# A decoder block's feed-forward down product: 16 of 22 row tiles by Strassen's seven block products, with sums of weight blocks kept in DRAM

## The chip, the cores and the metric

One core of one Trainium2 chip runs the whole kernel in one launch. The time is device time in microseconds. Before the change the median of three runs is 962.39 us, lowest 961.94 and highest 962.43. The engines are named as the profile names them: PE (TensorE), DVE (VectorE), ACT (ScalarE), POOL (GpSimd) and SP (SyncE, which here only issues DMAs).

## The reference

One layer of a hybrid decoder block for 512 tokens of width 1024, everything in float32:

```python
mod = cs @ ada_w[l] + ada_b[l]                       # cs = silu(c)
sh_m, sc_m, gt_m, sh_f, sc_f, gt_f = jnp.split(mod, N_MOD, axis=-1)
h = modulate(rmsnorm(x, norm_mix_g[l]), sh_m, sc_m)
proj = h @ w_in[l]                                   # q k v g_ret b_cv c_cv u_cv g_a g_b
...
y_a = (jax.nn.silu(g_ret) * y_ret) @ ret_w_out[l]    # retention branch
y_b = (b_cv * conv) @ conv_w_out[l]                  # short convolution branch
merged = jax.nn.sigmoid(g_a) * y_a + jax.nn.sigmoid(g_b) * y_b
x = x + gt_m[:, None, :] * (merged @ mix_w_out[l])
h = modulate(rmsnorm(x, norm_ffn_g[l]), sh_f, sc_f)
f = (jax.nn.silu(h @ ffn_w_gate[l]) * (h @ ffn_w_up[l])) @ ffn_w_down[l]
x = x + gt_f[:, None, :] * f
return rmsnorm(x, final_norm_g)
```

The feed-forward is 2816 wide, which is 22 row tiles of 128 of `ffn_w_down`. The change concerns the last matrix product, `f`, and when the vector `gt_f` is made.

## The kernel before

Each float32 operand is split into a high and a low part (`w_..._h`, `w_..._l`), and each product is three matmuls: low by high, high by low, high by high. A weight goes through four steps. SP's queue loads 1 MB into a `raw` buffer (`load_raw`, tag "raw", three buffers for the whole kernel); ACT casts a half of it to the high part; DVE subtracts to get the low part (`split`: tags "hi" and "lo", four buffers each); PE multiplies. SP's DMAs are issued in one order (`issue_after(load_raw.last...)`), so a load that waits for a free buffer holds back all behind it.

The stages of the code that matter here, in their order:

- The merge, two loops of four steps. A step of the first loop has the products `p_ga` and `p_ya` (loads `w_ga`, `w_ya`) and a part of the modulation for the feed-forward: `ada_load` fetches two buffers `ada_f` in eight DMAs of 256 KB, `mod_vecs` sums their rows on DVE (`acc_f`, eight operations) and four short matmuls turn the sum into columns. A step of the second loop has `p_gb` and `p_yb` (loads `w_gb`, `w_yb`). In its first step `gate_vec("gt_m")` starts: in four pieces, 1 MB of `ada_gt_m` is summed over rows on DVE (`acc_gt_m`, eight operations), split (`gh`, `gl`), and spread over the partitions by two matmuls (`gp_gt_m`). The pieces are taken at later points of the code (`after`, `tick`).
- `mix`: the merged product with `mix_w_out`, the residual sum into `x1` (`dx_gt_m`), and the feed-forward's norm, whose order is written out by hand on PE, DVE and ACT (`strict`): `n2s` to `n_r`, its reciprocal, `xn`, transposes `tx`, `h`, `Gh` and `Gl`.
- The feed-forward in two parts of 12 and 10 row tiles (`PARTS`). `swiglu` yields two tiles of silu(gate) × up for each 1 MB of `w_fg` and of `w_fu`; each tile is split (`fa_h`, `fa_l`). `tm_gemm` then multiplies them, tokens on the output's partitions, with two halves of 512 columns of `ffn_w_down` (`w_dn`, four row tiles in 1 MB) into four PSUM banks `dn`, and `add_gated` multiplies by `gt_f` and adds to `x1`. `gate_vec("gt_f")` starts at the third pair of tiles of the first part.

Of the kernel before, what the change touches and what calls it, by code (L numbers as in the profile page):

```python
# [19 lines left out]
P = 128  # L20
# [50 lines left out]
def block_kernel(ctx, tc, x, c, positions, ada_w, ada_b, norm_mix_g, w_in, conv_w, ret_w_out,  # L71
# [165 lines left out]
    def mod_vecs(f, j):  # L237

        pt = aux(f"mod_{f}{j}")
        a = ada_sum(ada_raw.pop((f, j)), 4 * P, f"{f}{j}")  # L240
        for i in range(4):
            mm(pt[:, i:i + 1], lhsT=a[:, i * P:(i + 1) * P], rhs=ones32[:, 0:1],
               start=True, stop=True)
        mod_cols(f, j, pt)
# [541 lines left out]
    def gate_vec(name):
        gate[name] = [misc(f"{name}_{h}") for h in range(2)]
        for h in range(2):
            with tc.issue_after(load_raw.last.ins):
                nc.sync.dma_start(  # L790
                    gate[name][h],
                    ada_b[0, ADA[name] + h * S:ADA[name] + (h + 1) * S].partition_broadcast(P))
        parts = {}

        def summed(j):
            raw = wp.tile([P, KT, 2 * P], F32, tag="raw", bufs=3, name=f"ada_{name}{j}")
            col = ADA[name] + 2 * j * P
            load_raw.last = nc.sync.dma_start(raw, aw[:, :, col:col + 2 * P])
            a = ada_sum([raw[:, k] for k in range(KT)], 2 * P, f"{name}{j}")
            gh = sp.tile([P, 2 * P], F32R, tag="gh", bufs=1, name=f"gh_{name}{j}")  # L800
            gl = sp.tile([P, 2 * P], F32R, tag="gl", bufs=1, name=f"gl_{name}{j}")
            parts[j] = split_act(a, "", gh, gl)

        def spread(j):
            gh, gl = parts.pop(j)
            pt = aux(f"gp_{name}{j}")
            mm(pt[:, 0:2 * P], lhsT=onesr, rhs=gl, start=True, stop=False)
            mm(pt[:, 0:2 * P], lhsT=onesr, rhs=gh, start=False, stop=True)
            gv = gate[name][j // 2][:, (j % 2) * 2 * P:(j % 2 + 1) * 2 * P]
            vec.tensor_tensor(gv, gv, pt[:, 0:2 * P], ALU.add)  # L810

        for j in range(4):
            after(2 * j + 1, lambda j=j: summed(j))
            after(2 * j + 2, lambda j=j: spread(j))

    for p in range(KT // 2):
        sg = {}
        for i, pt in proj(wi, COL["gb"] + 2 * p * P, Hh, Hl, f"gb{p}"):
            sg[i] = scr(f"sgb{p}{i}")
            act.activation(sg[i], pt, AF.Sigmoid)  # L820
        for i, pt in proj(conv_w_out[0], 2 * p * P, conv_in, None, f"yb{p}"):
# [48 lines left out]
    def add_gated(t, h, pt, g, cs=slice(0, S)):  # L870
        d = scr(f"dx_{g}{t}{h}_{cs.start}")[:, cs]
        vec.tensor_tensor(d, pt[:, cs], gate[g][h][:, cs], ALU.mult)
        vec.tensor_tensor(x1[t][h][:, cs], x1[t][h][:, cs], d, ALU.add)
# [133 lines left out]
    def swiglu(col):  # L1007
        if col == 0:
            for i, pg, pu in first_ffn():
                g = scr(f"fg{col}_{i}")  # L1010
                act.activation(g, pg, AF.Silu)
                vec.tensor_tensor(g, pu, g, ALU.mult)
                yield split_act(g, f"fa{i}")
            return
        gg = {}
        for i, pt in proj(ffn_w_gate[0], col, Gh, Gl, f"fg{col}"):
            gg[i] = scr(f"fg{col}_{i}")
            act.activation(gg[i], pt, AF.Silu)
        for i, pt in proj(ffn_w_up[0], col, Gh, Gl, f"fu{col}"):
            vec.tensor_tensor(gg[i], pt, gg[i], ALU.mult)  # L1020
            yield split_act(gg[i], f"fa{col}_{i}")

    o2 = out[0].rearrange("(t p) (h n) -> t h p n", p=P, n=S)
    ss3 = [sp.tile([P, 3], F32, tag="ss3", name=f"nfs_{t}") for t in range(NT)]
    PARTS = ((0, 12), (12, 10))
    for part, (f0, nf) in enumerate(PARTS):
        af = []
        for q in range(nf // 2):
            af += swiglu((f0 + 2 * q) * P)
            if part == 0 and q == 2:  # L1030
                gate_vec("gt_f")
        for h in range(2):
            groups = [acc(f"dn{part}{h}_{t}") for t in range(NT)]
            if part == 1 and h == 0:
                fg = [misc(f"fg_{i}") for i in range(2)]
                for i in range(2):
                    with tc.issue_after(load_raw.last.ins):
                        nc.sync.dma_start(
                            fg[i], final_norm_g[i * S:(i + 1) * S].partition_broadcast(P))
            if part == 0 or h == 0:  # L1040
                for t in tm_gemm(ffn_w_down[0], af, f0, nf, h, groups, nf - 4, f"dn{part}"):
                    add_gated(t, h, groups[t], "gt_f")
                    if part == 1:
                        half_ss(x1[t][h], ss3[t], h, f"nf_{t}")
                        vec.tensor_scalar(ss3[t][:, 0:1], ss3[t][:, 0:1], 1.0 / D, EPS, ALU.mult,
                                          ALU.add)
                        vec.tensor_tensor(x1[t][h], x1[t][h], fg[h], ALU.mult)
                continue
            groups.append(aux("dn_last"))
            xg = {}  # L1050
            for t, cs in tm_gemm(ffn_w_down[0], af, f0, nf, h, groups, nf - 6, f"dn{part}", True):
                add_gated(t, h, groups[NT if cs.start else t], "gt_f", cs)
                half_ss(x1[t][h][:, cs], ss3[t], 1 + cs.start // HS, f"nf_{t}")
                if cs.start == 0:
                    xg[t] = scr(f"xg_{t}")
                if cs.stop < S:
                    vec.scalar_tensor_tensor(ss3[t][:, 0:1], ss3[t][:, 1:2], 1.0 / D,
                                             ss3[t][:, 0:1], ALU.mult, ALU.add)
                vec.tensor_tensor(xg[t][:, cs], x1[t][h][:, cs], fg[h][:, cs], ALU.mult)
                if cs.stop < S:  # L1060
                    continue
                r = sp.tile([P, 1], F32, tag="rr", name=f"nf_{t}_r")
                i = 1 + cs.start // HS
                act.activation(r, ss3[t][:, i:i + 1], AF.Sqrt, scale=1.0 / D, bias=ss3[t][:, 0:1])
                vec.reciprocal(r, r)
                for i in (1, 0):
                    o = scr(f"o_{t}{i}")
                    if i:
                        vec.tensor_scalar_mul(o, xg[t], r)
                    else:  # L1070
                        act.mul(o, x1[t][0], r)
                    (nc.sync if i or t < NT - 1 else nc.scalar).dma_start(o2[t, i], o)


# [33 lines left out]
```

## Time and profile before

| | before |
|---|---|
| median of 3 runs | 962.39 us |
| the profiled execution's own time | 962.06 us |
| its span | 960.3 us |
| TensorE's granted clock, mean | 0.998 |
| PE busy | 949.9 us, 99% |
| DVE busy | 555.9 us, 58% |
| ACT busy | 340.1 us, 35% |
| POOL busy | 10.1 us, 1% |
| DMA, mean over the span | 126 GB/s |

Busy time is what an engine spends in instructions; shares are of the span. Times of instructions are counted from the span's start. The chain of work that ended last is followed back from the last instruction, and a row of it gives a start, a length, the engine, the tile written, the line and how many instructions in a row. DMA rows give the size of one transfer and the median time from its issue to its landing; the name before "DMA_DIRECT2D" is the queue that issued it.

### The profile page before, as it was taken

The page shows a single profiled execution, that of the slowest core. Times are in us where ns is not written, and L with a number is a line of the kernel's source. Part 1 is how long each engine was busy: PE and PEld are TensorE (multiplying, and loading weights), DVE is VectorE, ACT ScalarE, POOL GpSimd, SP SyncE. Part 2 cuts the span into 40 slices and gives each one's busy share as a digit, 9 for nine tenths or more (in the row PEclk, how much of TensorE's full clock was granted, in tenths as well). Part 3 has the DMA queues.
Part 4 walks back from the last instruction along what each step waited for, and adds up shares of the span by engine and source line. Part 5 has one row for each costly group of instructions (what it writes and reads, how often), then busy time and mean ns, then how long its engine had stood idle before and what let it go on. Part 6 is the DMA issues. An engine that isn't in the chain of part 4 may idle for free.

```text
span 960.3 us, 11325 instructions
## 1 busy us (share of the span) xinstructions
PE 949.9 (99%) x4619; PEld 802.7 (84%) x4619; DVE 555.9 (58%) x843; ACT 340.1 (35%) x505; POOL 10.1 (1%) x20
## 2 busy tenths in 40 slices
PE   8999999999999999999999999999999999999997
PEld 8898889888888888888888888888888888888886
DVE  5988875959674855554574358346533443333354
ACT  7534434444443423222232336333222122322223
POOL 2002000000000000000000000000000000000000
PEclk9999999999999999999999999999999999999999
DMA  9944223141222246764553640445433223332302
GB/s 308 343 146 133 80 96 99 56 143 56 88 88 88 77 127 189 209 188 154 175 175 101 206 132 15 140 132 175 133 116 103 87 88 93 122 114 66 110 1 88
DMA packets 109045, 120.98 MB, mean 126 GB/s; under 512 B 3701, under 2 KB 96929, under 8 KB 108993
## 3 DMA queue, kind: packets, MB, share of 16 engines
q1 hardware_dynamic: 108624, 119.82, 39.8%
q8 instruction: 36, 0.59, 0.3%
q0 software_dynamic: 224, 0.18, 0.1%
q10 hardware_dynamic: 144, 0.26, 0.1%
q14 instruction: 17, 0.13, 0.0%
HBM read 118.15 MB, written 2.10 MB: 125 GB/s over the span
## 4 chain that ended last, share of the span: by engine, by line
PE 96%; DVE 2%; ACT 1%; DMA 1%; issue 0%; SPq 0%; ACTq 0%
PE p_fu L64 13%; PE p_fg L64 12%; PE dn L64 12%; PE p_v L64 5%; PE p_ga L64 5%; PE p_gb L64 5%; PE p_yb L64 5%; PE p_ya L64 5%; PE p_k L64 4%; PE p_q L64 4%; PE p_g L64 3%; PE p_u L64 3%; PE p_b L64 3%; PE p_c L64 3%; PE mix L64 3%; PE mix L62 2%
## 5 line engine op out<-in xcount | busy, mean ns | idle before, releaser
L64 PE MATMUL dn<-w_dn_h,fa_l 128*128 128x512 f32 (+1 forms) x176 | 67.5, 384 | 0.0
L64 PE MATMUL dn<-w_dn_l,fa_h 128*128 128x512 f32 (+1 forms) x176 | 67.5, 383 | 0.0
L64 PE MATMUL dn<-w_dn_h,fa_h 128*128 128x512 f32 (+1 forms) x176 | 67.4, 383 | 0.0
L64 PE MATMUL p_fu<-Gh,w_fu_l 128*128 128x512 f32 x160 | 62.3, 389 | 0.0
L64 PE MATMUL p_fg<-Gh,w_fg_l 128*128 128x512 f32 x160 | 62.3, 389 | 0.0
L64 PE MATMUL p_fg<-Gh,w_fg_h 128*128 128x512 f32 x160 | 62.3, 389 | 0.0
L64 PE MATMUL p_fu<-Gh,w_fu_h 128*128 128x512 f32 x160 | 62.3, 389 | 0.0
L64 PE MATMUL p_fg<-Gl,w_fg_h 128*128 128x512 f32 x160 | 62.2, 389 | 0.0
L64 PE MATMUL p_fu<-Gl,w_fu_h 128*128 128x512 f32 x160 | 62.2, 389 | 0.0
L64 DVE TENSOR_TENSOR w_dn_l<-w_dn,w_dn_h 128x1024 fp32r<-128x1024 f32 x22 | 26.9, 1225 | 57.3 <-ACT w_dn_h L64 57.3
L64 DVE TENSOR_TENSOR w_fg_l<-w_fg,w_fg_h 128x1024 fp32r<-128x1024 f32 x20 | 24.4, 1224 | 56.5 <-ACT w_fg_h L64 56.5
L64 ACT CAST w_fu_h<-w_fu 128x1024 fp32r<-128x1024 f32 x20 | 21.1, 1053 | 74.2 <-PE p_fu L64 41.8
L64 ACT CAST w_dn_h<-w_dn 128x1024 fp32r<-128x1024 f32 x22 | 23.1, 1049 | 65.6 <-PE dn L64 39.4
L64 DVE TENSOR_TENSOR fg<-p_fu,fg 128x512 f32<-128x512 f32 x22 | 15.2, 691 | 49.6 <-PE p_fu L64 49.6
L64 ACT ACTIVATE fg<-p_fg 128x512 f32<-128x512 f32 x22 | 13.2, 598 | 78.0 <-PE p_fg L64 78.0
L64 PEld LDWEIGHTS dn<-w_dn_h,fa_l 128*128 128x128 f32 x176 | 33.1, 188 | 6.7 <-DVE dx_gt_f L64 0.2
L64 PEld LDWEIGHTS dn<-w_dn_h,fa_h 128*128 128x128 f32 x176 | 33.1, 188 | 6.5
L64 PEld LDWEIGHTS dn<-w_dn_l,fa_h 128*128 128x128 f32 x176 | 33.1, 188 | 6.4
L64 PE MATMUL p_v<-w_v_h,Hh 128*128 128x256 f32 x128 | 36.2, 283 | 0.0
L64 PE MATMUL p_v<-w_v_l,Hh 128*128 128x256 f32 x128 | 36.2, 283 | 0.0
L64 PE MATMUL p_v<-w_v_h,Hl 128*128 128x256 f32 x128 | 36.2, 283 | 0.0
L64 PEld LDWEIGHTS p_fg<-Gh,w_fg_h 128*128 128x128 f32 x160 | 30.0, 188 | 6.3
(373 smaller groups left out, 2536.1 us busy)
## 6 DMA issues: line engine op xcount, KB each, us to landing
w_fg<-in_ffn_w_gate_dram SPq DMA_DIRECT2D x11, 1024.0 KB, 5.5
w_fu<-in_ffn_w_up_dram SPq DMA_DIRECT2D x11, 1024.0 KB, 5.5
w_dn<-in_ffn_w_down_dram SPq DMA_DIRECT2D x10, 1024.0 KB, 5.1
ada_m<-in_ada_w_dram SPq DMA_DIRECT2D x32, 256.0 KB, 6.0
ada_f<-in_ada_w_dram SPq DMA_DIRECT2D x32, 256.0 KB, 4.9
w_v<-in_w_in_dram SPq DMA_DIRECT2D x4, 1024.0 KB, 6.8
w_q<-in_w_in_dram SPq DMA_DIRECT2D x4, 1024.0 KB, 5.1
w_g<-in_w_in_dram SPq DMA_DIRECT2D x4, 1024.0 KB, 5.1
```

The costliest lines, as they stand in the source:

```text
L62: self.last = op(*args, **kw)
L64: self.last = op(*args, **kw)
```

## The change

The 22 row tiles are now done in three parts of 8, 8 and 6. For the first two, the product A·B (A the activations, B the weights) is cut into 2 × 2 blocks: 256 tokens by four row tiles of A, four row tiles by 512 columns of B. Seven block products stand for eight, with sums of blocks of A (s1 to s4) and of B (t1 to t4) as factors, and sums of the products (u2, u3) on the way to the output. The last six tiles go the old way.

The sums of B don't depend on the data, but on the weights alone; they are made in the merge loops: each of the eight steps loads two row tiles of `ffn_w_down` into a `raw` buffer (`w_bl`), takes four differences on DVE in place, and writes the buffer to DRAM (`blocks`) by a DMA of POOL's queue. Eight of the fourteen block products then load their weights from `blocks`, six from `ffn_w_down`. The sums of A are made on DVE as the second half of a part's tiles comes out of `swiglu`. `gate_vec("gt_f")` starts after the first pair of tiles in place of the third.

```diff
+    dp = ctx.enter_context(tc.tile_pool(name="dp", bufs=1, space=bass.MemoryType.DRAM))
...
+    PARTS = ((0, 8), (8, 8), (16, 6))
+    blocks = [dp.tile([P, nf // 2, 2, D], F32, tag="blocks", bufs=2, name=f"blocks{i}")
+              for i, (_, nf) in enumerate(PARTS[:2])]
+
+    def block_sums():
+        for part, (f0, nf) in enumerate(PARTS[:2]):
+            for k in range(nf // 2):
+                w = wp.tile([P, 2, D], F32, tag="raw", bufs=3, name=f"w_bl{part}{k}")
+                for i in range(2):
+                    r0 = (f0 + k + i * nf // 2) * P
+                    with tc.issue_after(load_raw.last.ins):
+                        load_raw.last = nc.sync.dma_start(w[:, i], ffn_w_down[0, r0:r0 + P, :])
+                (b11, b12), (b21, b22) = ([w[:, i, j * S:(j + 1) * S] for j in range(2)]
+                                          for i in range(2))
+                vec.tensor_tensor(b11, b12, b11, ALU.subtract)
+                vec.tensor_tensor(b12, b22, b12, ALU.subtract)
+                vec.tensor_tensor(b22, b22, b11, ALU.subtract)
+                vec.tensor_tensor(b21, b21, b22, ALU.subtract)
+                nc.gpsimd.dma_start(blocks[part][:, k], w)
+                yield
+
+    block_steps = block_sums()
...
         ada_load("f", 2 * p)
         mod_vecs("f", 2 * p)
+        next(block_steps)
...
         if p == 0:
             gate_vec("gt_m")
+        next(block_steps)
...
+    def block_acts(part, nf):
+
+        first, acts = [], {n: [] for n in ("a11", "a12", "a22", "s1", "s2", "s3", "s4")}
+        tok = slice(0, HS), slice(HS, S)
+        f0 = PARTS[part][0]
+        for q in range(nf // 2):
+            for g in swiglu((f0 + 2 * q) * P):
+                if len(first) < nf // 2:
+                    k = len(first)
+                    t = misc(f"a11_{part}{k}", F32R)
+                    acts["a11"].append(split_act(g[:, tok[0]], "", t[:, tok[0]], t[:, tok[1]]))
+                    first.append(g)
+                    continue
+                k = len(acts["s1"])
+                a11, a21 = (first[k][:, i] for i in tok)
+                a12, a22 = (g[:, i] for i in tok)
+                sums = [scr(f"s{part}{k}_{i}") for i in range(2)]
+                (s1, s2), (s3, s4) = ([s[:, i] for i in tok] for s in sums)
+                both = [split_act(g, f"a2_{part}{k}")]
+                vec.tensor_tensor(s1, a21, a22, ALU.add)
+                vec.tensor_tensor(s2, s1, a11, ALU.subtract)
+                vec.tensor_tensor(s3, a11, a21, ALU.subtract)
+                vec.tensor_tensor(s4, a12, s2, ALU.subtract)
+                both += [split_act(s, f"s{part}{k}{i}") for i, s in enumerate(sums)]
+                for i, n in enumerate(("a12", "a22", "s1", "s2", "s3", "s4")):
+                    acts[n].append([z[:, tok[i % 2]] for z in both[i // 2]])
+            if part == 0 and q == 0:
+                gate_vec("gt_f")
+        return acts
+
+    def block_weights(part, n):
+
+        f0, nf = PARTS[part]
+        h = nf // 2
+        t = {"t1": (0, 0), "t3": (0, 1), "t4": (1, 0), "t2": (1, 1)}.get(n)
+        if t is None:
+            i, j = int(n[1]) - 1, int(n[2]) - 1
+            raw = load_raw(ffn_w_down[0], f0 + i * h, h, j * S, S, f"w_{n}{part}")
+        else:
+            raw = wp.tile([P, h, S], F32, tag="raw", bufs=3, name=f"w_{n}{part}")
+            with tc.issue_after(load_raw.last.ins):
+                load_raw.last = nc.sync.dma_start(
+                    raw, blocks[part][:, :, t[0], t[1] * S:(t[1] + 1) * S])
+        ws = [split(raw[:, k:k + 2, :], [P, 2, S], f"w_{n}{part}{k}") for k in range(0, h, 2)]
+        return [[w[:, k % 2, :] for w in ws[k // 2]] for k in range(h)]
+
+    def block_product(pts, acts, ws):
+        h = len(ws)
+        for i, pt in enumerate(pts):
+            ts = slice(i * P, (i + 1) * P)
+            for k, ((ah, al), (wh, wl)) in enumerate(zip(acts, ws)):
+                mm(pt, lhsT=al[:, ts], rhs=wh, start=k == 0, stop=False)
+                mm(pt, lhsT=ah[:, ts], rhs=wl, start=False, stop=False)
+                mm(pt, lhsT=ah[:, ts], rhs=wh, start=False, stop=k == h - 1)
+            yield i, pt
+
+    def add_gated_sum(t, h, pt, u):
+        d = scr(f"du_{t}{h}")
+        vec.tensor_tensor(d, pt, u, ALU.add)
+        vec.tensor_tensor(d, d, gate["gt_f"][h], ALU.mult)
+        vec.tensor_tensor(x1[t][h], x1[t][h], d, ALU.add)
+
+    def block_down(part, acts):
+
+        def product(bank, a, w):
+            pts = [bank(f"dn{part}_{w}{i}") for i in range(2)]
+            yield from block_product(pts, acts[a], block_weights(part, w))
+
+        u2, u3 = {}, {}
+        for i, pt in product(acc, "a11", "b11"):
+            u2[i] = scr(f"u2_{part}{i}")
+            act.copy(u2[i], pt)
+        for i, pt in product(acc, "a12", "b21"):
+            add_gated_sum(i, 0, pt, u2[i])
+        for i, pt in product(pv, "s2", "t2"):
+            vec.tensor_tensor(u2[i], pt, u2[i], ALU.add)
+        for i, pt in product(aux, "s3", "t3"):
+            u3[i] = scr(f"u3_{part}{i}")
+            vec.tensor_tensor(u3[i], pt, u2[i], ALU.add)
+        for i, pt in product(acc, "s1", "t1"):
+            add_gated_sum(2 + i, 1, pt, u3[i])
+            vec.tensor_tensor(u2[i], pt, u2[i], ALU.add)
+        for i, pt in product(acc, "s4", "b22"):
+            add_gated_sum(i, 1, pt, u2[i])
+        for i, pt in product(pv, "a22", "t4"):
+            add_gated_sum(2 + i, 0, pt, u3[i])
...
-    PARTS = ((0, 12), (12, 10))
-    for part, (f0, nf) in enumerate(PARTS):
-        af = []
-        for q in range(nf // 2):
-            af += swiglu((f0 + 2 * q) * P)
-            if part == 0 and q == 2:
-                gate_vec("gt_f")
...
+    for part in range(2):
+        block_down(part, block_acts(part, PARTS[part][1]))
+
+    f0, nf = PARTS[2]
+    af = []
+    for q in range(nf // 2):
+        af += [split_act(g, f"fa{q}") for g in swiglu((f0 + 2 * q) * P)]
...
```

The last part is the old loop body for one part, with its names shortened. Three places show how this moves instructions. In each row there are the source line, the operation, the tile written, the tiles read, the shape, and how many alike follow each other.

SP's queue in the first steps of the first merge loop, before (`w_ya` in four DMAs, `ada_f` in eight):

```order
L107 DMA w_ga_3294<-in_w_in_dram 128x8x256
L764 DMA w_ya_3358<-in_ret_w_out_dram 64x4x256 x4
L64 DMA ada_f_0_3423<-in_ada_w_dram 128x2x256 x4
L64 DMA ada_f_4_3428<-in_ada_w_dram 128x2x256 x4
L107 DMA w_ga_3450<-in_w_in_dram 128x8x256
L764 DMA w_ya_3514<-in_ret_w_out_dram 64x4x256 x4
L64 DMA ada_f_0_3579<-in_ada_w_dram 128x2x256 x4
```

The same place now:

```order
L108 DMA w_ga_3298<-in_w_in_dram 128x8x256
L791 DMA w_ya_3362<-in_ret_w_out_dram 64x4x256 x4
L64 DMA ada_f_0_3427<-in_ada_w_dram 128x2x256 x4
L64 DMA ada_f_4_3432<-in_ada_w_dram 128x2x256 x4
L756 DMA w_bl_3454<-in_ffn_w_down_dram 128x1024 x2
L108 DMA w_ga_3462<-in_w_in_dram 128x8x256
L791 DMA w_ya_3526<-in_ret_w_out_dram 64x4x256 x4
L64 DMA ada_f_0_3591<-in_ada_w_dram 128x2x256 x4
```

Each block's load stands behind the step's `ada_f` and ahead of the next step's `w_ga`; the next step's first `ada_f` buffer is the one that the block is written from. In the second loop a block's load stands ahead of the next `w_gb`, and the last one ahead of the first `w_mix`.

DVE at the first token tile of the feed-forward's norm (`n2s` holds the sums of squares, `n_0_r` the root), before:

```order
L62 TENSOR_TENSOR x_0_1_4543<-x_0_1_4543,dx_gt_m_0_4770 128x512
L62 TENSOR_TENSOR n_0_r<-n2s_4560 128x1
L62 RECIPROCAL n_0_r<-n_0_r 128x1
L62 TENSOR_SCALAR xn_00_4779<-x_0_0_4542,n_0_r 128x512
L62 TENSOR_SCALAR xn_01_4781<-x_0_1_4543,n_0_r 128x512
```

And now:

```order
L62 TENSOR_TENSOR x_0_1_4611<-x_0_1_4611,dx_gt_m_0_4838 128x512
L62 TENSOR_TENSOR n_0_r<-n2s_4628 128x1
L64 TENSOR_SCALAR acc_gt_f_5295<-ada_gt_f_5293,cs 128x256
L64 SCALAR_TENSOR_TENSOR acc_gt_f_5295<-ada_gt_f_5293,cs,acc_gt_f_5295 128x256 x3
L62 RECIPROCAL n_0_r<-n_0_r 128x1
L64 SCALAR_TENSOR_TENSOR acc_gt_f_5295<-ada_gt_f_5293,cs,acc_gt_f_5295 128x256
L62 TENSOR_SCALAR xn_00_4847<-x_0_0_4610,n_0_r 128x512
L62 TENSOR_SCALAR xn_01_4849<-x_0_1_4611,n_0_r 128x512
```

Sums of the first piece of `gt_f` stand between the steps of the norm, and with them the wait for `ada_gt_f` to land.

DVE at the end of the first part's tiles, where the first block products begin (`fg` a tile of silu(gate) × up, `s` sums of A, `w_b` weights from `ffn_w_down`, `w_t` weights from `blocks`):

```order
L64 TENSOR_TENSOR w_b_l<-w_b_5834,w_b_h 128x1024
L64 TENSOR_TENSOR s_l<-s_1_5727,s_h 128x512
L64 TENSOR_TENSOR fg_1_5692<-p_fu_5748,fg_1_5692 128x512
L64 TENSOR_TENSOR s_0_5774<-fg_1_5337,fg_1_5692 128x256
L64 TENSOR_TENSOR s_1_5775<-fg_1_5337 128x256
L64 TENSOR_TENSOR s_0_5774<-s_0_5774,fg_1_5337 128x256
L64 TENSOR_TENSOR a_03_l<-fg_1_5692,a_03_h 128x512
L64 TENSOR_TENSOR s_1_5775<-fg_1_5692,s_0_5774 128x256
L64 TENSOR_TENSOR s_l<-s_0_5774,s_h 128x512
L64 TENSOR_TENSOR w_b_l<-w_b_5834,w_b_h 128x1024
L64 TENSOR_TENSOR s_l<-s_1_5775,s_h 128x512
L64 TENSOR_TENSOR w_t_l<-w_t_5878,w_t_h 128x1024 x2
```

And at the end of that part's block products:

```order
L64 TENSOR_TENSOR w_t_l<-w_t_6046,w_t_h 128x1024
L64 TENSOR_TENSOR x_0_1_4611<-x_0_1_4611,du_6024 128x512
L64 TENSOR_TENSOR du_6040<-dn_b_6001,u_01_5830 128x512
L64 TENSOR_TENSOR w_fg_l<-w_fg_6088,w_fg_h 128x1024
L64 TENSOR_TENSOR du_6040<-du_6040,gt_f_5257 128x512
L64 TENSOR_TENSOR du_6068<-dn_t_6044,u_00_5938 128x512
L64 TENSOR_TENSOR x_1_1_4613<-x_1_1_4613,du_6040 128x512
```

The splits of the first two products' weights stand among the last tiles of gate and up (the first product's two just ahead of the rows shown), and the splits of the next gate and up weights among the last sums; before, the same place has two operations (`dx_gt_f`, `x`) for each of eight output tiles, and the splits of `w_dn`.

More of the change, by code (lines that the diff above doesn't have):

```diff
@@ L1012, in swiglu @@
                 vec.tensor_tensor(g, pu, g, ALU.mult)
-                yield split_act(g, f"fa{i}")
+                yield g
             return
@@ L1020, in swiglu @@
             vec.tensor_tensor(gg[i], pt, gg[i], ALU.mult)
-            yield split_act(gg[i], f"fa{col}_{i}")
+            yield gg[i]
+    def block_acts(part, nf):
[26 more added lines that the diff above has]
+        return acts
@@ L1023, in block_kernel @@
     o2 = out[0].rearrange("(t p) (h n) -> t h p n", p=P, n=S)
     ss3 = [sp.tile([P, 3], F32, tag="ss3", name=f"nfs_{t}") for t in range(NT)]
-    PARTS = ((0, 12), (12, 10))
-    for part, (f0, nf) in enumerate(PARTS):
-        af = []
-        for q in range(nf // 2):
-            af += swiglu((f0 + 2 * q) * P)
-            if part == 0 and q == 2:
-                gate_vec("gt_f")
[L1032 to L1047, printed above, removed]
-                continue
[L1049 to L1072, printed above, removed]
@@ new lines, in block_kernel @@
+    for part in range(2):
[4 more added lines that the diff above has]
+        af += [split_act(g, f"fa{q}") for g in swiglu((f0 + 2 * q) * P)]
+    for h in range(2):
+        groups = [acc(f"dn{h}_{t}") for t in range(NT)]
+        if h == 0:
+            fg = [misc(f"fg_{i}") for i in range(2)]
+            for i in range(2):
+                with tc.issue_after(load_raw.last.ins):
+                    nc.sync.dma_start(
+                        fg[i], final_norm_g[i * S:(i + 1) * S].partition_broadcast(P))
+            for t in tm_gemm(ffn_w_down[0], af, f0, nf, h, groups, nf - 4, "dn"):
+                add_gated(t, h, groups[t], "gt_f")
+                half_ss(x1[t][h], ss3[t], h, f"nf_{t}")
+                vec.tensor_scalar(ss3[t][:, 0:1], ss3[t][:, 0:1], 1.0 / D, EPS, ALU.mult, ALU.add)
+                vec.tensor_tensor(x1[t][h], x1[t][h], fg[h], ALU.mult)
+            continue
+        groups.append(aux("dn_last"))
+        xg = {}
+        for t, cs in tm_gemm(ffn_w_down[0], af, f0, nf, h, groups, nf - 6, "dn", True):
+            add_gated(t, h, groups[NT if cs.start else t], "gt_f", cs)
+            half_ss(x1[t][h][:, cs], ss3[t], 1 + cs.start // HS, f"nf_{t}")
+            if cs.start == 0:
+                xg[t] = scr(f"xg_{t}")
+            if cs.stop < S:
+                vec.scalar_tensor_tensor(ss3[t][:, 0:1], ss3[t][:, 1:2], 1.0 / D,
+                                         ss3[t][:, 0:1], ALU.mult, ALU.add)
+            vec.tensor_tensor(xg[t][:, cs], x1[t][h][:, cs], fg[h][:, cs], ALU.mult)
+            if cs.stop < S:
+                continue
+            r = sp.tile([P, 1], F32, tag="rr", name=f"nf_{t}_r")
+            i = 1 + cs.start // HS
+            act.activation(r, ss3[t][:, i:i + 1], AF.Sqrt, scale=1.0 / D, bias=ss3[t][:, 0:1])
+            vec.reciprocal(r, r)
+            for i in (1, 0):
+                o = scr(f"o_{t}{i}")
+                if i:
+                    vec.tensor_scalar_mul(o, xg[t], r)
+                else:
+                    act.mul(o, x1[t][0], r)
+                (nc.sync if i or t < NT - 1 else nc.scalar).dma_start(o2[t, i], o)
```

## The prediction

> **What bounds the kernel now.** I read the page first, for the engine that is full, then the chain of work that ended last, then the stretches of the span by window, and last the DMA issues and the waits of the stages in which the new loads are placed.
>
> ```profile
> span 960.3 us, 11325 instructions
> PE 949.9 (99%) x4619; PEld 802.7 (84%) x4619; DVE 555.9 (58%) x843; ACT 340.1 (35%) x505; POOL 10.1 (1%) x20
> PEclk9999999999999999999999999999999999999999
> GB/s 308 343 146 133 80 96 99 56 143 56 88 88 88 77 127 189 209 188 154 175 175 101 206 132 15 140 132 175 133 116 103 87 88 93 122 114 66 110 1 88
> ```
>
> TensorE is busy for 99% at a full clock. So every matmul that goes is worth its whole time, if TensorE doesn't begin to wait. The chain of work shows where it stands, with its start and length:
>
> ```profile
> 366.02 10.88 PE p_ga L64 x48
> 388.56 11.00 PE p_ga L64 x48
> ...
> 433.88 11.00 PE p_ga L64 x48
> ...
> 456.54 11.00 PE p_gb L64 x48
> ...
> 522.98 10.91 PE p_gb L64 x48
> ...
> 544.76 27.20 PE mix L64 x120
> ...
> 724.76 65.28 PE dn L64 x288
> ```
>
> A dn matmul takes 65.28/288 = 0.2267 us. One step of the first merge loop (p_ga, p_ya, the modulation columns) is (456.54 − 366.02)/4 = 22.6 us, one of the second loop (p_gb, p_yb) is (522.98 − 456.54)/3 = 22.15 us. The new loads go into these eight steps. The windows give each step's busy time of PE, PEld, DVE, ACT and POOL, the clock, the DMA share and GB/s:
>
> ```profile
> 366.00:388.00 22.00, 22.00 (x102) 18.26 (x100) 12.34 (x17) 7.17 (x9) 0.00 (x0) 1.00 0.70 190
> 388.00:411.00 23.00, 23.00 (x110) 19.26 (x109) 12.35 (x18) 5.52 (x7) 0.00 (x0) 1.00 0.71 185
> 411.00:434.00 23.00, 23.00 (x107) 19.25 (x108) 12.24 (x19) 5.51 (x7) 0.00 (x0) 1.00 0.73 198
> 434.00:456.00 22.00, 22.00 (x101) 18.26 (x100) 8.36 (x14) 4.51 (x7) 0.00 (x0) 1.00 0.45 152
> 456.00:478.00 22.00, 22.00 (x100) 18.32 (x101) 12.66 (x23) 5.99 (x8) 0.00 (x0) 1.00 0.53 168
> 478.00:500.00 22.00, 22.00 (x99) 18.23 (x98) 15.80 (x27) 6.67 (x9) 0.00 (x0) 1.00 0.58 189
> 725.00:790.00 65.00, 65.00 (x288) 53.83 (x288) 24.18 (x28) 13.02 (x13) 0.00 (x0) 1.00 0.31 97
> ```
>
> The reader is to see that TensorE never waits there, but that the DMA engines are busy for 0.70 to 0.73 of the first three steps, against 0.31 in the down products. The waits say the same: VectorE and the SP queue stand waiting for ada_f to land.
>
> ```profile
> DVE acc_f L64 <- DMA ada_f<-in_ada_w_dram: 24.1, 10, 6.3
> SPq L64 <- DMA ada_f<-in_ada_w_dram: 21.9, 9, 5.9
> ```
>
> **The change, part by part.** The sum stands against the profiled run's own 962.06 us (span 960.3 and 1.8 around it); the median of the runs is 962.39, 0.3 above, which I add at the end.
>
> *Removed.* For eight row tiles the old way has 8 × 4 × 2 × 3 = 192 matmuls, seven block products have 7 × 2 × 4 × 3 = 168. Two such parts save 48 matmuls: 48 × 0.2267 = **−10.9 us**.
>
> *The block products themselves.* One product is 24 matmuls, 5.44 us, and seven are 38.1 us. The rows for what VectorE and ScalarE do beside them:
>
> ```profile
> L64 DVE TENSOR_TENSOR w_dn_l<-w_dn,w_dn_h 128x1024 fp32r<-128x1024 f32 x22 | 26.9, 1225 | 57.3 <-ACT w_dn_h L64 57.3
> L64 ACT CAST w_dn_h<-w_dn 128x1024 fp32r<-128x1024 f32 x22 | 23.1, 1049 | 65.6 <-PE dn L64 39.4 <-issue 17.4 <-PE p_fu L64 7.7
> L64 DVE TENSOR_TENSOR x<-x,dx_gt_f 128x512 f32<-128x512 f32 x15 | 10.4, 691 | 0.4
> L64 DVE TENSOR_TENSOR sm<-st,dec 128x256 f32<-128x256 f32 x8 | 3.4, 420 | 0.3 <-PE st L64 0.2
> ```
>
> VectorE has 14 splits × 1.225 = 17.2 us and 30 sums (eight calls of three, six into u2 and u3) × 0.69 = 20.7 us: 37.9 of 38.1. The order on VectorE puts the first four splits (4.9) ahead of the products, under gate and up, and four splits of the next gate and up weights (4.9) into them, so the load stays 37.9. I take 0, hidden by the products with hardly anything to spare; ScalarE, with 14 × 1.05 and a few copies, has room. The seven 1 MB weight loads per part raise DMA from 0.31 to about 0.31 × (7/38.1)/(6/65.3) = 0.62. The activation sums cost four VectorE operations of 0.42 and two further splits of 0.69 for each second-half tile, 3.1 us; the last tile's sums aren't wanted until two products (10.9 us) have run. 0 as well.
>
> *The block sums: eight more turns of a ring of three buffers.* All weights come through three 1 MB buffers, loaded in order by SP's queue. Each step now loads a block of 1 MB, takes four VectorE sums, and holds the buffer until POOL's queue has written 1 MB to DRAM. The next load into that buffer (ada_f's first half, in the second loop ada_gt_m or a weight) stands in SP's queue behind this, and every later load behind it.
>
> ```profile
> w_dn<-in_ffn_w_down_dram SPq DMA_DIRECT2D x10, 1024.0 KB, 5.1
> ada_f<-in_ada_w_dram SPq DMA_DIRECT2D x32, 256.0 KB, 4.9
> w_ga<-in_w_in_dram SPq DMA_DIRECT2D x4, 1024.0 KB, 8.0
> w_gb<-in_w_in_dram SPq DMA_DIRECT2D x4, 1024.0 KB, 5.9
> ada_gt_m<-in_ada_w_dram SPq DMA_DIRECT2D x4, 1024.0 KB, 6.6
> ada_gt_f<-in_ada_w_dram SPq DMA_DIRECT2D x4, 1024.0 KB, 6.7
> out_dram<-o SPq DMA_DIRECT2D x7, 256.0 KB, 2.3
> posi<-in_positions_dram POOLq DMA_DIRECT2D x2, 64.0 KB, 6.1
> ...
> L64 DVE SCALAR_TENSOR_TENSOR acc_f<-ada_f,cs,acc_f 128x512 f32<-128x512 f32 x28 | 21.0, 751 | 11.3 <-DMA ada_f<-in_ada_w_dram 10.6
> ...
> L64 DVE SCALAR_TENSOR_TENSOR acc_gt_m<-ada_gt_m,cs,acc_gt_m 128x256 f32<-128x256 f32 x28 | 13.6, 484 | 0.9
> ```
>
> No row shows a 1 MB write W to DRAM, nor one by POOL's queue. From below: SP writes 256 KB in 2.3, and the other 786 kB at 343 GB/s take 2.3, so 4.6 us. From above I take POOL's 6.1 for next to nothing, 983 kB at 308 GB/s (3.2), and the 2.9 us by which a 1 MB load is stretched at 0.70 DMA share (w_ga 8.0 against w_dn 5.1): 12.2. I take **8.7**, between the middle of these ends (8.4) and POOL's own row without the stretch (6.1 and 983 kB at 343 GB/s: 9.0), which is the nearest: the same queue, and also in a stretch of busy DMA, though it is a read.
>
> The Trainium skill bears on this price: its page DMA: Bandwidth & Descriptors, section Anatomy of one DMA — SWDGE (gpsimd) path, gives about 2.0 us plus the bytes at 436 GB/s. By it W would be an estimated 4.4 us, under my lower end; POOL's row of 6.1 us for 64 KB doesn't agree with so small a fixed part. By that price the sum would come out as in the first rival below. The same page, section Issuing engines are not separate DMA queues, says that a DMA of another engine's queue shares the same 16 engines; the 0.70 share here can't show it for POOL, since POOL moves nothing in these steps.
>
> Are the DMA engines enough? 0.70 to 0.73 of a step are 16 us; 2.1 MB more at 308 to 343 GB/s are 6.1 to 6.8: 22 to 23 of 22.6. In the first three steps they are full, so a block's load takes w_ga's 8.0 there, and 6.3 (between w_gb and ada_gt_m) later.
>
> First loop: 8.0 + 4 × 0.69 + 8.7 + 4.9 (ada_f) + 2 × 0.75 = 25.9, which is 3.2 longer than the step; three times 9.7, and the fourth with 6.3 adds 1.5: 11.2 us late. Second loop: 6.3 + 2.8 + 8.7 + 6.6 + 0.35 + 7 × 0.484 = 28.1 against 22.15, 6.0 late each. Against this stands the lead of the loads, from SP's own rows:
>
> ```profile
> 494.09 0.38 SPq L107 DMA_DIRECT2D w_gb<-in_w_in_dram  x1
> ...
> 514.76 22.35 SPq L107 DMA_DIRECT2D w_mix<-in_mix_w_out_dram  x3
> ...
> 569.32 0.37 SPq L107 DMA_DIRECT2D w_fu<-in_ffn_w_up_dram  x1
> ```
>
> The last w_gb is issued at 494.09, lands 5.9 later, is cast and split in 1.05 + 1.22, and is wanted at 522.98: a lead of 20.7. Three turns of the second loop stand before it: 11.2 + 17.9 = 29.1 late, so TensorE waits 8.4 in the gb stage. The first w_mix (lead 544.76 − 514.76 − 5.0 − 2.3 = 22.7) has a fourth turn before it: 35.0 − 22.7 = **12.3 us** of waiting in all, of which 3.9 fall to the mix stage. Behind the late block and ada loads on VectorE stand the splits of the next weights, so the late load and the late split are one wait and not two.
>
> *gate_vec moved.* Its first ada_gt_f load takes the place in SP's queue of the w_fu at 569.32, and lands 6.7 later, at 576.0. On VectorE its products now stand inside the first norm of the feed-forward:
>
> ```profile
> 574.27 0.16 DVE L62 TENSOR_TENSOR n_r<-n2s 128x1 f32<-128x1 f32 x1 [0.85 <-ACT n_j L62]
> 575.88 0.17 DVE L62 RECIPROCAL n_r<-n_r 128x1 f32<-128x1 f32 x1 [1.45 <-ACT n_r L62]
> 576.08 0.88 DVE L62 TENSOR_SCALAR xn<-x,n_r 128x512 f32<-128x512 f32 x2
> ```
>
> Four stand between the sum and the reciprocal (0.35 + 3 × 0.484 = 1.8 us), a fifth before xn. If the load is early, 1.45 us of them fall into the wait for ScalarE and 0.8 is left; if it lands at 576.0, xn comes 2.4 later. Behind xn TensorE's transposes and the rest of the mix products wait. I take the middle, **+1.6**.
>
> *Other edits.* The moved gate rows, 16 more issues on SP (0.4 to 0.5 each) and eight on POOL, which stands idle, cost nothing of their own: the queue's waits above cover them.
>
> Sum: 962.06 − 10.9 + 12.3 + 1.6 = 965.1, and with 0.3 for the median 965.4 us.
>
> **The rivals.** *The ring has slack (faster).* The lateness has eight times W in it, less where a loop is shorter than its step. With W at 7.2 or less the 35.0 fall by 8 × 1.5 = 12 to about the lead of 22.7, and nothing is left but the norm: 962.4 − 10.9 + 0.8 to 2.4 = 952.3 to 953.9. For it speaks that SP's write takes only 2.3 us for 256 KB; against it the full DMA engines. At W = 8.3 (31.9 late, 9.2 of waiting, 1.6 for the norm) stalls and gain are equal, and the time is that of before. Here the price by the skill's page named above would also lead.
>
> *The write is slow and everything is stretched.* With W = 11.6 (8.7 and w_ga's 2.9) the first loop is 28.8, 6.2 too long, 23 late after four; the second is 6.0 to 8.9 too long, 24 to 36 after four. Of these 47 to 59 less the lead a wait of 24 to 36 is left, and 977 to 989 us. For it speaks DVE's 24.1 us of waits for ada_f already; against it that a waiting TensorE gives the queue time to catch up.
>
> *VectorE becomes the bound in the block products.* If the splits done ahead are not done ahead, its load per part is 42.8 against 38.1: 4.7 us each, 9.4 in both, which nearly eats the gain: 961 with no ring cost. Against it stands the order on VectorE.
>
> **How the numbers follow.** A measurement of this kernel can tell about 0.2% (1.9 us) from no change. My forecast (ring late, 964.4 to about 975): 0.40. Slack (952 to 956): 0.28, and a partial gain up to 960.4, with the VectorE case in part: 0.07. Level, 960.5 to 964.3: 0.13. Slow write, over 975: 0.12. So faster 0.35, same 0.13, slower 0.52. For 8 in 10 the range goes from 952.3, the slack ring, to 977, where the slow write begins; the likeliest case's own range is 964 to 975.
>
> **What would show it.** In the changed profile: 480 dn matmuls at 0.227; POOL's writes with 8 to 9 us to landing; DMA share near 1 in 366 to 434; waits of TensorE on p_gb and mix weights, 8 and 4 us; SP waiting on blocks; the reciprocal in the first feed-forward norm about 2 us later. No wait of TensorE in the block products. Wrong: if writes land in under 7 us and TensorE doesn't wait between 450 and 560, the gain is whole; if TensorE waits on dn products' weights, VectorE was the bound.

## The result and the profile after

The changed kernel takes 965.08 us (963.81 to 966.15, six runs) against 961.91 before: a ratio of 1.0031, 95% interval 1.0019 to 1.0043. It is slower by 3.2 us; 965.4 was forecast. The profiled execution took 966.15 us, its span is 963.7.

From the page of the changed kernel, the span, busy times, and the chain that ended last by engine:

```profile
span 963.7 us, 11476 instructions
PE 943.4 (98%) x4559; PEld 795.4 (83%) x4559; DVE 631.6 (66%) x979; ACT 362.5 (38%) x537; POOL 14.4 (1%) x28
PE 74%; DMA 12%; DVE 10%; ACT 2%; issue 1%; SPq 1%; DVEq 0%; ACTq 0%
```

TensorE is busy 6.5 us less, and no longer alone on the chain: 12% of it are now DMAs, 10% VectorE. The chain in order of time shows where:

```profile
372.12 6.40 DMA blocks<-w_bl
...
397.63 7.43 DMA blocks<-w_bl
...
423.35 7.76 DMA blocks<-w_bl
...
448.85 8.75 DMA blocks<-w_bl
458.03 4.50 DMA w_bl<-in_ffn_w_down_dram
465.06 4.13 DMA blocks<-w_bl
469.25 8.40 DMA ada_gt_m<-in_ada_w_dram
480.55 1.22 DVE w_gb_l L64
...
557.75 18.56 PE mix L64 x82
...
695.93 10.88 PE dn_b L64 x48
...
734.01 10.88 PE p_fg L64 x48
```

Three readings. The block products take 734.01 − 695.93 = 38.08 us per part, with no gap. The mix starts at 557.75 against 544.76, 13.0 late, although the second merge loop began on time (456.2 against 456.4). And through the merge loops the chain runs over the blocks' writes, and at the first long wait over ada_gt_m and a split on VectorE. TensorE's waits (total, times, longest):

```profile
PE gp_gt_m L64 <- DVE gl_gt_m L64: 5.6, 2, 4.5
PE p_gb L64 <- DVE w_gb_l L64: 3.6, 1, 3.6
...
PE tx L62 <- DVE xn L62: 1.0, 1, 1.0
...
PE p_fg L64 <- DVE Gl L62: 0.5, 1, 0.5
```

The first two rows are 9.2 us in the second loop, not 13.0. Most of the rest is in TensorE's rows behind the two long waits (start, length, and in brackets the wait):

```profile
481.82 0.50 PE L64 MATMUL p_gb<-Hh,w_gb_l 128*128 128x512 f32 x1 [3.56 <-DVE w_gb_l L64]
...
483.63 0.63 PE L64 MATMUL p_gb<-Hh,w_gb_l 128*128 128x512 f32 x1
484.06 0.63 PE L64 MATMUL p_gb<-Hl,w_gb_h 128*128 128x512 f32 x1
...
510.31 0.55 PE L64 MATMUL gp_gt_m<-gl_gt_m,onesr 128*128 128x256 f32 x1 [4.54 <-DVE gl_gt_m L64]
```

For some 3 us a matmul follows the last after 0.43 us in place of 0.227, which loses about 1.6 us behind each of these two waits. The windows (columns as in the prediction: PE, PEld, DVE, ACT, POOL, clock, DMA share, GB/s) show it as the granted clock, 0.92 and 0.93:

```profile
434.00:456.00 22.00, 22.00 (x102) 18.30 (x101) 14.29 (x21) 4.56 (x7) 0.53 (x1) 1.00 0.87 278
456.00:478.00 22.00, 22.00 (x100) 18.16 (x99) 6.88 (x12) 2.33 (x3) 0.53 (x1) 1.00 0.74 252
478.00:500.00 22.00, 18.43 (x76) 14.87 (x75) 17.77 (x31) 5.47 (x8) 0.00 (x0) 0.92 0.43 146
500.00:523.00 23.00, 18.46 (x76) 14.83 (x74) 13.66 (x25) 5.62 (x8) 0.53 (x1) 0.93 0.67 229
```

What TensorE waited for stands on VectorE's timeline, and on SP's queue below it:

```profile
477.68 0.35 DVE L64 TENSOR_SCALAR acc_gt_m<-ada_gt_m,cs 128x256 f32<-128x256 f32 x1 [9.13 <-DMA ada_gt_m<-in_ada_w_dram]
478.07 2.57 DVE L64 SCALAR_TENSOR_TENSOR acc_gt_m<-ada_gt_m,cs,acc_gt_m 128x256 f32<-128x256 f32 x5
480.55 1.22 DVE L64 TENSOR_TENSOR w_gb_l<-w_gb,w_gb_h 128x1024 fp32r<-128x1024 f32 x1
```
```profile
444.52 0.38 SPq L108 DMA_DIRECT2D w_gb<-in_w_in_dram  x1
...
458.56 0.38 SPq L108 DMA_DIRECT2D w_gb<-in_w_in_dram  x1
469.25 0.59 SPq L826 DMA_DIRECT2D ada_gt_m<-in_ada_w_dram  x1
...
525.84 0.38 SPq L108 DMA_DIRECT2D w_gb<-in_w_in_dram  x1
...
546.79 9.31 SPq L108 DMA_DIRECT2D w_mix<-in_mix_w_out_dram  x3
```

The weights for the late p_gb were issued at 458.56, 19 us before TensorE wanted them. Their split stood on VectorE behind sums of ada_gt_m, issued only at 469.25, when a block's write (465.06 and 4.13) had ended. From 350 to 560 us SP's queue waits 56.8 us in all for writes of blocks.

### The profile page after: what moved, and what is told of

It reads as the page before. It is cut to its first block, busy times and chain, and to the rows that moved or that the text cites. A ratio compares the mean times of both kernels' runs of the same rounds, so it can differ in the third digit from the quotient of the medians.

```text
span 963.7 us, 11476 instructions
## 1 busy us (share of the span) xinstructions
PE 943.4 (98%) x4559; PEld 795.4 (83%) x4559; DVE 631.6 (66%) x979; ACT 362.5 (38%) x537; POOL 14.4 (1%) x28
## 4 chain that ended last, share of the span: by engine, by line
PE 74%; DMA 12%; DVE 10%; ACT 2%; issue 1%; SPq 1%; DVEq 0%; ACTq 0%
PE p_fu L64 12%; PE p_fg L64 12%; PE p_v L64 5%; PE dn_t L64 5%; PE p_k L64 4%; PE p_q L64 4%; DMA blocks<-w_bl 4%; PE p_g L64 3%; PE p_c L64 3%; PE dn_b L64 3%; PE dn L64 3%; PE p_u L64 2%; DMA ada_f<-in_ada_w_dram 2%; PE p_b L64 2%; PE p_yb L64 2%; DMA ada_gt_m<-in_ada_w_dram 2%
## 5 line engine op out<-in xcount | busy, mean ns | idle before, releaser
L64 DVE TENSOR_TENSOR w_b_l<-w_b,w_b_h 128x1024 fp32r<-128x1024 f32 x18 | 22.0, 1222 | 29.1 <-ACT w_b_h L64 29.1
L64 PEld LDWEIGHTS p_fu<-Gh,w_fu_h 128*128 128x128 f32 x160 | 30.0, 188 | 6.2
L64 PEld LDWEIGHTS p_fu<-Gl,w_fu_h 128*128 128x128 f32 x160 | 30.0, 188 | 6.2
L64 PEld LDWEIGHTS p_fg<-Gl,w_fg_h 128*128 128x128 f32 x160 | 30.0, 188 | 6.2
L64 PEld LDWEIGHTS p_fu<-Gh,w_fu_l 128*128 128x128 f32 x160 | 30.0, 188 | 6.2
L64 PEld LDWEIGHTS p_fg<-Gh,w_fg_l 128*128 128x128 f32 x160 | 30.0, 188 | 6.1
L64 DVE TENSOR_TENSOR w_bl<-w_bl 128x512 f32<-128x512 f32 x32 | 22.0, 688 | 14.2 <-DMA w_bl<-in_ffn_w_down_dram 13.8
L64 PE MATMUL p_gb<-Hh,w_gb_l 128*128 128x512 f32 x64 | 26.3, 411 | 3.6 <-DVE w_gb_l L64 3.6
```

The lines of the kernel that those rows point to most:

```text
L64: self.last = op(*args, **kw)
```

## The experiments

Times are medians beside the kernel before on the same chip (961.8 to 962.0).

**1. The block sums left out (e1_strassen_no_sums).**

```diff
-        next(block_steps)
...
-                load_raw.last = nc.sync.dma_start(
-                    raw, blocks[part][:, :, t[0], t[1] * S:(t[1] + 1) * S])
+            raw = load_raw(ffn_w_down[0], f0 + t[0] * h, h, t[1] * S, S, f"w_{n}{part}")
```

> The block sums are left out: the eight products that need sums of weight blocks read plain blocks of ffn_w_down instead (so their numbers are others), everything else as in the changed kernel. Theory (the ring of three weight buffers is held up by the blocks, and the waits of 13 us in the second merge loop eat the gain): no wait on p_gb or gp_gt_m is left, 961.9 - 11.5 (what the trace shows between the two profiles from the gate and up products on) + 2 (norm) = 952 to 953 us. Rival (the block products themselves, or VectorE in them, give back the gain): 958 us or more.

952.46 us, ratio 0.9903 (0.9886 to 0.9919). The seven products give their gain; the loss comes with making the sums.

**2 and 3. The block steps alone, on the kernel before; with and without the write (e2_sums_only, e3_sums_no_write).**

```diff
+        next(block_steps)          # at the end of each merge step; PARTS and down product as before
...
-                nc.gpsimd.dma_start(blocks[part][:, k], w)      # only in e3
```

> The kernel before with the eight block steps added in the merge loops; the blocks are written to DRAM and not used. Theory: the whole price of the block steps, 13 us in the second merge loop, without the gain: 974 to 976 us. Rival (the loss lies in the block products or in the moved gate_vec): 966 us or less.

> As the one with the block steps alone, without POOL's write of the block: the loads and the four sums stay. Theory (the hold of a ring buffer until the write lands, 6.9 us of a loop of 25.5, is what makes the loads late): loop 18.6 us, under the step's 22.6, and 962 to 965 us. Rival (the extra load and its place in SP's queue, or VectorE's sums, cost the time): 970 us or more.

972.71 us (1.0114, 1.0099 to 1.0129) and 962.07 us (1.0001, 0.9992 to 1.0010). The steps cost 10.7 us, and all of it goes with the write: eight more loads of 1 MB and 32 more sums on VectorE cost nothing that can be measured, though the first w_gb is issued 10.2 us later than before (435.23 against 425.07). With 2 as the price and 1 as the gain, 1.2 us of loss would follow, and 3.2 were measured; these 2 us, in the same waits (9.2 against 6.7), stay unexplained.

**4. Buffers of their own (e4_own_buffers).**

```diff
-                w = wp.tile([P, 2, D], F32, tag="raw", bufs=3, name=f"w_bl{part}{k}")
+                bl = [[misc(f"w_bl{part}{k}_{i}{j}") for j in range(2)] for i in range(2)]
```

> The changed kernel with the blocks in four tiles of their own (256 KB each, from a pool that is idle in the merge loops) in place of a buffer of the ring; as many bytes are loaded and written, in four loads and four writes of POOL's queue per step. Theory (ring): the loads of weights and ada are on time again, no wait in the second merge loop, 952 to 955 us. Rival (the DMA engines are full, whoever holds a buffer): waits stay, 962 to 966 us.

966.25 us (1.0043, 1.0028 to 1.0058): no gain, against the theory. The first w_gb is issued at 433.3, against 444.5 in the changed kernel and 425.1 before, so the ring is relieved. Loads that meet the writes land late all the same (first the DMA row, then TensorE's waits):

```profile
ada_gt_m<-in_ada_w_dram SPq DMA_DIRECT2D x4, 1024.0 KB, 9.0
```
```profile
PE gp_gt_m L64 <- DVE gl_gt_m L64: 4.2, 2, 4.0
PE p_gb L64 <- DVE w_gb_l L64: 4.1, 2, 2.3
PE p_yb L64 <- DVE w_yb_l L64: 1.9, 1, 1.9
```

There is only one set of these buffers, so that a step also waits for the write of the step before (SP's four loads of a block take 8.58 us to issue at 442.74). This run doesn't part the two causes; the next two do.

**5 and 6. Bytes without a held buffer, and a held buffer without bytes (e5_traffic_no_hold, e6_hold_tiny), both on the kernel before.** The lines are shown against those of e2.

```diff
-                nc.gpsimd.dma_start(blocks[part][:, k], w)
+                pool.tensor_tensor(t, w[:, 1, 0:16], w[:, 1, 16:32], ALU.subtract)      # e5
+                    nc.gpsimd.dma_start(blocks[part][:, k]..., Hh[:, 0:4, :]...)
...
+                nc.gpsimd.dma_start(blocks[part][:, k, 1, 0:16], w[:, 1, 0:16])         # e6
```

> The kernel before with the block steps, where POOL writes 1 MB to DRAM after each block's sums, but out of a tile that stays in place (the normed activations' high part) and not out of the ring's buffer: the same bytes at the same time, and the buffer is free after the sums and a small operation of POOL that reads 16 columns. What is written is not the block. Theory (a held buffer): 961.5 to 964 us, as without a write. Rival (1 MB of writes slows the loads of the others): 968 to 973 us, as with the blocks' own write (972.7).

> The kernel before with the block steps, where POOL writes only 16 of a block's 2048 columns (8 KB for 1 MB) out of the ring's buffer. Theory (hold): the time follows the time to landing of so small a write; with 2 to 3 us the loop is 20.6 to 21.6 us, under the step, and the time 962 to 964; with 5 to 6, as POOL's small loads at the start show, it is 23.6 to 24.6, and 965 to 970. Rival (bytes): 962 whatever its landing.

970.72 us (1.0090, 1.0073 to 1.0107) and 963.58 us (1.0020, 1.0006 to 1.0034; single runs from 961.6 to 968.2). The bytes alone, with no buffer held for them, make 8.9 us, against 10.7 with the hold; a buffer held for a small write costs 1.8. So most of the loss needs no held buffer. What a hold of the full length would cost without its bytes was not run. In the DMA rows of e3 and then of e5 the same load takes longer, and in e5's waits from 440 to 540 us VectorE waits for it (13.9 us in e3, the longest 4.2):

```profile
ada_gt_m<-in_ada_w_dram SPq DMA_DIRECT2D x4, 1024.0 KB, 5.6
```
```profile
ada_gt_m<-in_ada_w_dram SPq DMA_DIRECT2D x4, 1024.0 KB, 7.8
blocks<-Hh POOLq DMA_DIRECT2D x8, 1024.0 KB, 7.3
```
```profile
DVE acc_gt_m L64 <- DMA ada_gt_m<-in_ada_w_dram: 22.9, 4, 7.0
```

Beside the first ada_gt_m of e5 (8.33 us, issued at 456.68) a write is on its way, issued at 456.87; a window over the two:

```profile
456.70:465.00 8.30, 8.30 (x38) 6.90 (x37) 1.33 (x2) 1.53 (x2) 0.56 (x1) 1.00 0.95 335
```

The DMA engines are busy for 0.95 of it, with the load and the write both on their way. Not every load is stretched: w_ga and w_gb land in 5.0 and 5.1 us in e3 and in 5.1 in e5. The small write of e6 lands in 3.6 us, so that its hold is about half as long as that of a whole block.

**7 and 8. The block steps moved ahead of the merge loops (e7_early), and gate_vec later (e8_early_gate_late).**

```diff
             act.activation(gg[i], pt, AF.Silu)
+        next(block_steps)                      # retention steps 1 to 4; four more in the conv steps
...
-            if part == 0 and q == 0:           # e8
+            if part == 0 and q == 1:
```

> The changed kernel with the eight block steps moved to the stages ahead of the merge loops: one after each of the four retention steps, four in the conv projections. There the DMA engines are 0.2 to 0.4 busy, and a buffer's turn is 12 us or longer. Theory: no waits in the merge loops, the norm's 1.6 stays: 952 to 954 us. Rival (VectorE is 0.7 to 0.9 busy in the retention steps, and its queue is held by the block's loads): 956 us or more.

> As the one with the early block steps, and gate_vec for gt_f starts after the second pair of tiles of the first part in place of the first, so that its sums don't stand in the norm. Theory: the norm's waits (1.0 on xn, 0.6 on Gl) go: 950.5 to 952 us. Rival (gt_f comes too late for the first block products): waits of TensorE or no gain against the early steps alone, 953 us or more.

958.84 us (0.9969, 0.9960 to 0.9979) and 956.88 us (0.9945, 0.9931 to 0.9960). Both are faster than before, but short of the forecast. The merge loops have no waits now; a new one stands in the first retention step. The wait, and then rows of e7's chain ahead of it:

```profile
PE p_g L64 <- DVE k_b L64: 4.1, 1, 4.1
```
```profile
80.29 1.13 DVE w_q_l L64
81.44 7.41 DMA w_v<-in_w_in_dram
88.95 1.05 ACT w_v_h L64
```

Before, SP issued this w_v at 59.19. Now the block takes that place in the ring of three buffers (59.95) and keeps it until its write, issued at 92.49, has ended, so that w_v goes out when w_q's split frees a buffer, at 81.44. ScalarE's queue stands behind its cast, and with it the sines and cosines for k_b. VectorE's own last angles are also later, at 88.30 in place of 85.04, behind the block's sums; no run parts the two. Here a place in the ring counts, and not only bytes.

Between the two runs lie 2.0 us, and the later gate_vec is worth that much: from the first mix matmul to the first p_fg of 48 e7 takes 71.9 us, e8 70.1, as before (614.89 − 544.76). In e8 the waits on xn and Gl are gone.

**9. The steps spread over stages with room (e9_spread).**

```diff
-        next(block_steps)                      # not after the first retention step
+        if p in (1, 2, 3):
+            next(block_steps)
...
+            if (part, q) in ((0, 2), (0, 3)):  # two in gate and up; three in the conv steps
+                next(block_steps)
```

> The block steps away from the merge loops and from the first retention step, where the early version showed TensorE waiting 4 us for VectorE: one after each of retention steps 2 to 4, one in each of the three later conv steps, two in the gate and up products of the first part; gate_vec after the second pair of tiles. Theory (the loss is made only where 1 MB of writes meets loads that VectorE's queue waits for at once): 950 to 952.5 us, as without sums at all (952.5) or a little less. Rival (each block step costs some time wherever it stands): 954 us or more.

952.15 us, ratio 0.9898 (0.9883 to 0.9912): 9.9 us faster than before, 12.9 faster than the changed kernel, with the same bytes. From its DMA rows:

```profile
blocks<-w_bl POOLq DMA_DIRECT2D x8, 1024.0 KB, 4.2
```

TensorE no longer waits in the merge loops. But gate_vec starts a pair of tiles later here too, which is worth 2.0. Against e1 (952.46, gate_vec early and no sums) the spread steps thus still cost an estimated 1.7 us; the mix starts at 546.00 against 544.52 in e1.

**10. The write from ScalarE's queue (e10_write_act).**

```diff
-                nc.gpsimd.dma_start(blocks[part][:, k], w)
+                nc.scalar.dma_start(blocks[part][:, k], w)
```

> The changed kernel with the blocks written by ScalarE's queue in place of POOL's. As many bytes at nearly the same time. Theory now (the write's bytes share the DMA engines with the loads): 962 to 967 us, little changed. Rival (POOL's queue is slow): the write lands in 4 us or less, and the time falls to 953 to 958 us.

970.05 us (1.0080, 1.0062 to 1.0099). The write lands hardly earlier than from POOL (6.9), so POOL's queue isn't what is slow; and ScalarE now waits in order for a block's sums before it can issue. TensorE's waits in the merge loops and the mix are 11.6 us here, against 9.2:

```profile
blocks<-w_bl ACTq DMA_DIRECT2D x8, 1024.0 KB, 6.5
```
```profile
ACT sga L64 <- DVE w_bl L64: 35.3, 3, 13.3
```

**11. Block steps in the first merge loop only (e11_first_loop_only).**

```diff
             gate_vec("gt_m")
-        next(block_steps)
...
+            if (part, q) in ((0, 2), (0, 3), (1, 0), (1, 1)):
+                next(block_steps)
```

> The changed kernel with the four block steps of the second merge loop moved to the gate and up products; the four of the first loop stay. Theory: the loads leave the first loop some 20 us late, as in the changed kernel, which is about the lead of the second loop's loads; without more blocks there, TensorE waits 0 to 5 us: 952 to 957 us. Rival (the second loop's waits come from the lateness of the first): 962 us or more.

958.31 us (0.9957, 0.9942 to 0.9971), between the two theories: moving the second loop's four blocks away is worth 6.8 us, and the first loop's, with their lateness, still leave a wait of 2.3.

**12. As many bytes read in place of written (e12_reads_no_hold, on the kernel before).** The lines are shown against those of e2.

```diff
-                nc.gpsimd.dma_start(blocks[part][:, k], w)
+                            nc.gpsimd.dma_start(m, ffn_w_down[0, r0:r0 + P, j * S:(j + 1) * S])
```

> The kernel before with the block steps, where POOL's queue after each block's sums loads 1 MB (four pieces of 256 KB) from DRAM into tiles that nothing reads, in place of writing 1 MB: as many bytes at the same time, but reads, and no buffer of the ring is held. The blocks are not written. Theory (bytes on shared DMA engines, whichever way they go): 968 to 972 us, as with a write from a tile outside the ring (970.7). Rival (a write to DRAM slows the loads in a way of its own): 962 to 965 us.

973.69 us (1.0118, 1.0101 to 1.0134): reads cost 11.7 us, the writes of e5 8.9. So it isn't something that only writes do, but 1 MB more moved at that moment. The busy DMA engines (0.95 in e5's window) speak for a meeting there; no run parts them from DRAM behind them.

## Why the prediction was right, and where its steps were not

The time, 965.4 against 965.08, is right, and so is the place; that it is so near is partly luck, as misses of opposite sign met. In the spans, the terms measure −11.6, +13.0 and +2.0, which is 963.7 − 960.3. Term by term:

- *Gain of the products, −10.9.* Held. From the first p_fg of 48 (629.85, before 614.89) to the end the changed profile is 11.6 us shorter, 0.7 more than the 48 matmuls, and without sums the whole kernel gains 9.5, about this gain less the norm's 2.0.
- *Block products, 0.* Held: 38.08 us of 38.1 and no wait. VectorE was to be the tightest, 37.9; it was busy 34.4 us of 38, so there was more to spare than forecast.
- *Norm, +1.6.* 2.0: from the first mix matmul to the first p_fg of 48 it is 72.10 us, 70.13 before. TensorE waits 1.0 on xn and 0.5 on Gl. The rows: from n_r to xn 2.91 us, 1.81 before, because four of the moved sums stand between.

```profile
587.27 0.16 DVE L62 TENSOR_TENSOR n_r<-n2s 128x1 f32<-128x1 f32 x1 [0.85 <-ACT n_j L62]
...
588.22 1.53 DVE L64 SCALAR_TENSOR_TENSOR acc_gt_f<-ada_gt_f,cs,acc_gt_f 128x256 f32<-128x256 f32 x3
589.66 0.15 DVE L62 RECIPROCAL n_r<-n_r 128x1 f32<-128x1 f32 x1
...
590.18 0.88 DVE L62 TENSOR_SCALAR xn<-x,n_r 128x512 f32<-128x512 f32 x2
```

- *Waits in the merge, +12.3.* 13.0, but made otherwise. The lateness at its end was near: the last w_gb 31.8 us late (525.84 − 494.09; 29.1 forecast), the first w_mix 32.0 (35.0). But the first w_gb was already 19.4 late (444.52 − 425.07) where 11.2 were forecast, and the second loop's three turns added 12.3 in place of 17.9; by then TensorE itself ran late. The split was not: 8.4 in the gb stage and 3.9 at mix were forecast, and all 13.0 fell in the gb stage.
- *The step that failed: the write's price as a hold and nothing else.* W was put at 8.7; the writes' median is 6.9 in the changed kernel:

```profile
w_bl<-in_ffn_w_down_dram SPq DMA_DIRECT2D x16, 512.0 KB, 4.9
blocks<-w_bl POOLq DMA_DIRECT2D x8, 1024.0 KB, 6.9
...
ada_gt_m<-in_ada_w_dram SPq DMA_DIRECT2D x4, 1024.0 KB, 7.4
```

By the prediction's own sum a W under 7.2 leaves no wait and a time of 952.3 to 953.9, and there were 9.2 us of waits. SP did wait for the blocks' writes, as forecast, but experiments 5 and 12 show that this isn't needed: a megabyte more, with no buffer held for it, costs 8.9 and 11.7 us, and a hold of 3.6 us without the bytes 1.8. I had the stretch in the block's load only (8.0; its two halves land in 4.9 each), and not in ada_gt_m, 7.4 here against 6.6 before and 5.6 in e3. Nor does the DMA share alone give a stretch: w_ga, 8.0 at shares of 0.70 to 0.73, lands in 5.1 in the changed kernel at 0.75 to 0.78. So W was too high, the slowing of other loads was left out, and the two misses had opposite signs.
- *"One wait and not two."* The late load and the late split were indeed one wait, but the load was that of ada_gt_m and not of the weights: VectorE's order, not the weights' lead of 20.7 us, set it. The DMA share was near 1 only in stretches: 0.75 to 0.78 over the windows from 366 to 434, but 0.94 to 0.97 while the first loop's four blocks are written (372.1 to 378.5 and so on), and 0.78 while VectorE waits for the late ada_gt_m (469.2 to 477.7). Behind that load stood a split whose high part had been cast at 466.62.
- *Not foreseen:* some 3.3 us of the 13.0 are lost to slow matmuls behind the two long waits.

The Trainium skill, page DMA: Bandwidth & Descriptors, section Anatomy of one DMA — SWDGE (gpsimd) path, gave an estimated 4.4 us for the write. The 4.2 of e9 agrees with it, and the 6.9 beside other loads does not; POOL's rows of 6.1 at the start, which I took as the nearest, were no measure of its queue. The same page of the Trainium skill, section Issuing engines are not separate DMA queues, says that DMAs of all issuing engines run on the same 16 engines and interleave; experiment 10 agrees with it (6.5 us from ScalarE's queue, 6.9 from POOL's).

## What to carry to other kernels

Price a new transfer by what it does to the ones beside it, not only by its own landing: look which loads an in-order engine waits for at that time, and what stands behind them on that engine. Count the places in a ring of buffers too: in e7 a block in the ring put a weight's load off by 22 us. Work that depends on weights alone can go to any stage; the same eight blocks cost 10.7 us in the merge loops and an estimated 1.7 in e9, spread over stages where the DMA engines have more room (seven of the eight writes run at shares of 0.58 to 0.78). Where TensorE does nearly all the time's work, a wait can cost more than its length: here about 1.6 us more behind waits of 3.56 and 4.54.

## What the hardware showed that was not expected

Matmuls ran at half pace after a wait of TensorE: 0.43 us from start to start in place of 0.227, for some 3 us, after waits of 3.56 and 4.54 us, and in e11 after one of 2.26. These are rows of e11; the wait ended at 513.47, so that the half pace began 1.3 us later:

```profile
514.74 0.61 PE L64 MATMUL p_yb<-ci_l,w_yb_h 128*128 128x512 f32 x1
515.15 0.63 PE L64 MATMUL p_yb<-ci_h,w_yb_h 128*128 128x512 f32 x1
515.58 0.63 PE L64 MATMUL p_yb<-ci_h,w_yb_l 128*128 128x512 f32 x1
```

The Trainium skill, page TensorE: Matmul & The Clock Gate, Part 1: The HAM clock gate (the "warmup" mystery), says that the array falls to half its clock after an idle window of about 3.4 us, and gives 426.7 ns from start to start at 512 columns. The pace agrees. The 2.26 us of e11 show that a wait shorter than the window can do it, and e4, where no slow matmuls follow a wait of 2.29, that it need not; in the second merge loop of e4 and e12 the waits of 1.67 to 1.87 us had none behind them.
